# Starting a 7-product block inside the output projection, with respaced attention steps and an earlier first down pass

## The chip, the core and the metric

The kernel runs on one core of a Trainium2 chip. The metric is the device time of one execution in microseconds. The core has TensorE (PE in the profile, its weight loads PEld), VectorE (DVE), ScalarE (ACT), GpSimd (POOL) and SyncE (SP, which here only issues DMAs). Each engine works through a queue of its own, and semaphores tie the queues together.

## The reference

Two decoder layers over 256 tokens of width 2048, all in float32. Cut to what matters:

```python
h = rms_norm(x, norm1_g[l])
z = h @ w_in[l]                              # 2048 x 3584: sgu u | sgu v | q | k | v
out_a = chunked_sgu(gelu(z_sgu), ...)        # 16 groups, 128 x 128 causal mixing per chunk
out_b = swa_sink_attention(q, k, v, ...)     # 16 heads, 4 key heads, window 128, sinks, bias
mixed = concat([rms_norm(out_a), rms_norm(out_b)])
x = x + mixed @ w_out[l]                     # 2048 x 2048
h2 = rms_norm(x, norm2_g[l])
x = x + (silu(h2 @ w_gate[l]) * (h2 @ w_up[l])) @ w_down[l]   # 2048 x 5632 twice, 5632 x 2048
```

## The kernel before

The 256 tokens are two tiles of 128 (t = 0, 1). Weights come in pieces of 256 rows by 512 columns, 512 KB each, into one of 7 buffers named raw. Each piece is split into two float32r parts: ACT casts the high part wh (L94, 5 buffers), DVE subtracts to get the low part wl (L95, 4 buffers). Every product is then three matmuls (mm3, L124 to L126): high by high, high by low, low by high.

An **ordinary unit** (`unit`, L128) is one piece against both token tiles: 12 matmuls of 512 columns. A **7-product unit** (`s_unit` in `seven`, L608) is one piece in a Strassen-like scheme for gate and up: 6 matmuls. Here a 2 x 2 arrangement of token halves and gate/up column blocks is computed in seven products instead of eight, for feed-forward blocks 1 to 10 of 11. A 7-product block has 28 units and 30 steps (a step is one `yield`). Its first 20 units come in four groups i = 0 to 3 of five; each group needs three pieces, three DVE additions (L636, L637, L640) and one accumulating load by POOL (L642) into the tile t2. Group i uses the transposed, normed activations pairs2[2i] and pairs2[2i+1], and the sums of them in ext2. The block accumulates in five PSUM tiles of pool pa (tag acc, named m in the profile). At its end come ACT and DVE steps that undo the scheme, the gating (`gated`, L659), and the transposes of the result (`act_T`, L584, named ps_f, then aT).

PSUM is shared by three pools: pa with 5 slots (tag acc), pd with 2 (tag dacc) and pm with 1. Small products and transposes take their slots by turns from pm, pd, pd, pa (`small_ps`, L119).

The order in which instructions are written is set by hand. `tick` (L107) advances a clock, by 1 for an ordinary unit and by 0.5 for a 7-product unit; `later(delay, fn)` (L104) runs fn at the first tick at or after its due time, and things due at one tick go by due time, then by the order of registration. The framework then plans each engine's queue from that written order and its own estimates, so instructions can run ahead of their written place.

A layer goes so:

- The input projection, seven blocks of 8 ordinary units, in the order k and v, two blocks of q, two of sgu v, two of sgu u. Between the units, by `later`, run the norms of k and q (`head_inv`, with a power on POOL, L171), their transposes (`to_T`), six attention pieces (`attend`, L322, at ticks 6, 9, 12, 15, 19 and 23 after the first q block), each with scores ps_s, then exps one tick later, then `turn` (transposes ps_p) three ticks later, then `weigh` (ps_v, then ob) five ticks later; the closing transposes of a head group (`attend_end`), and the spatial gate (`spatial`).
- The output projection, eight parts of four units (`add_part`, L555), in the order b0, b1, a0, a1, b2, a2, b3, a3: b is the attention half of the input, a the sgu half, the figure the block of 512 columns. Each accumulates in pa; DVE then adds the scaled result into xres (L559). After an a part the block's squares and transposes for the next norm follow (`norm_block`, L500, and `combine`, L474).
- The feed-forward: `s_stream` runs the ten 7-product blocks step by step, and `std_stream` (L785) offers ordinary units: gate and up of block 0 (`gate_up`, 16 units in pd), and passes of `down` over finished blocks, 8 units for each block. A loop at L802 puts ordinary units between the steps, 88 in 300 steps. `down` seeds its accumulators with xres (L721), multiplies, and drains them into xres (L746). It starts a pass when at least two finished blocks are there, or all that are left.

Of the kernel before, what the change touches and what calls it, by code (L numbers as in the profile page):

```python
# [20 lines left out]
P = 128  # L21
# [42 lines left out]
def trunk(ctx, tc, x, xt, w_in, w_out, w_gate, w_up, w_down, sgu_w, sgu_g, consts,  # L64
# [182 lines left out]
    for lay in range(L):  # L247
# [40 lines left out]
        def q_norm(b, acc, lay=lay, layer=layer, qT=qT):  # L288
            qn = []
            for t in range(NTOK):  # L290
                z = zp.tile([P, NB], F32, tag="z", name="zq")
                nc.scalar.activation(z, acc[t], AF.Copy, scale=layer["rstd1"][t])
                qn.append(z)

            def scaled(inv):
                for t in range(NTOK):
                    z3 = qn[t].rearrange("p (h d) -> p h d", d=HD)
                    nc.vector.tensor_tensor(z3, z3, bc(inv[t], HD), ALU.mult)
# [12 lines left out]

        ssb = small([P, NTOK, 2], "ssb")
        ob = {}
# [8 lines left out]
        def attend(gp, t, i0, n, zkv=zkv, kT=kT, qT=qT, ob=ob, bias=bias, layer=layer):  # L322
# [229 lines left out]
        pairs2 = []  # L552
        ext2 = []

        def add_part(n, pairs, chunks, kind):  # L555
            acc = product([w_out[lay, n, c] for c in chunks], pairs)
            for t in range(NTOK):
                xs = xres[:, t, n * NB : (n + 1) * NB]
                nc.vector.scalar_tensor_tensor(  # L559
                    xs, acc[t], rstds[kind][t], xs, ALU.mult, ALU.add  # L560
                )

        for part, n in (("b", 0), ("b", 1), ("a", 0), ("a", 1), ("b", 2), ("a", 2), ("b", 3), ("a", 3)):
            if part == "b":
                add_part(n, pairs_b, range(4, 8), part)
            else:
                add_part(n, pairs_a, range(4), part)
                norm_block(n, ss2, pairs2, lay, C_G2, ext2)
        rstd2 = finish_rms(ss2, D)

        nr = small([P, NTOK], "nr")
        nrstd2 = [nr[:, t : t + 1] for t in range(NTOK)]

        def negate(rstd2=rstd2, nrstd2=nrstd2):
            for t in range(NTOK):
                nc.vector.tensor_scalar(nrstd2[t], rstd2[t], -1.0, None, ALU.mult)

        later(2, negate)

        ss1 = small([P, NTOK, ND], "ss4")  # L580
        pairs1 = []
        pairs_f = {}
# [22 lines left out]

                later(2 + c, ready)

        def seven(b, lay=lay, pairs2=pairs2, ext2=ext2, act_later=act_later):  # L608
            bank = [pa.tile([P, NB], F32, tag="acc", name=f"m{i}") for i in range(5)]

            def s_unit(raw, m, i, op, first, last, bank=bank):
# [45 lines left out]
                nc.vector.tensor_tensor(out, x, y, ALU.add)  # L657

            def gated(t, psum, sg, c):  # L659
                nc.scalar.activation(sg, psum, AF.Silu, scale=rstd2[t])  # L660
                nc.vector.scalar_tensor_tensor(sg, c, nrstd2[t], sg, ALU.mult, ALU.mult)

            steps = {
                0: lambda: add(c21, bank[2], m0),
# [19 lines left out]
                yield from seven(b)  # L684

        seeds = []

        def even(b, w, lay=lay, pairs2=pairs2):
            acc = new_acc(pd, "dacc")
# [4 lines left out]
                    yield True  # L694
            return acc

        def gate_up(b, even=even, act_later=act_later, seeds=seeds):
            acc = yield from even(b, w_gate)
            sg = []
            for t in range(NTOK):  # L700
                s = zp.tile([P, NB], F32, tag="z", name="sg")
                nc.scalar.activation(s, acc[t], AF.Silu, scale=rstd2[t])
                sg.append(s)
            acc = yield from even(b, w_up)
            for t in range(NTOK):
                nc.vector.scalar_tensor_tensor(
                    sg[t], acc[t], rstd2[t], sg[t], ALU.mult, ALU.mult
                )
                later(1.5 + 0.5 * t, lambda t=t: seeds[0](0, t))
            act_later(b, sg)  # L710

        left = [NFF]

        accs = {}
        full = {}
# [69 lines left out]
        def std_stream(gate_up=gate_up, down=down, pairs_f=pairs_f, left=left):  # L785
            gus = list(GU_BLOCKS)
            downed = set()
            while left[0]:
                full = [b for b in sorted(pairs_f) if len(pairs_f[b]) == 2 and b not in downed]
                rest = left[0] == len(full)  # L790
                if len(full) >= CHUNK[0] or rest:
                    blocks = full[: CHUNK[1]]
                    downed.update(blocks)
                    yield from down(blocks)
# [2 lines left out]
                else:  # L797
                    yield False

        other = std_stream()  # L800
# [98 lines left out]
```

## Time and profile before

| | |
|---|---|
| median of 3 runs | 1940.1 us (1939.55 to 1940.67) |
| the profiled execution | 1940.95 us |
| its span, first to last instruction | 1939.2 us |
| PE busy | 1925.2 us (99%) |
| DVE busy | 1660.9 us (86%) |
| ACT busy | 1301.4 us (67%) |
| POOL busy | 123.2 us (6%) |
| DMA | 426.41 MB, 220 GB/s in the mean |
| mean granted clock of TensorE | 0.999 |

The busy time of PE is modelled from the starts of its matmuls, and the share is a mean over stages. A group's row gives line, engine, operation, output from inputs, shape and count, then busy us and mean ns of one, then the engine's idle time just before it and what ended it. A row of a timeline gives start and length in us, and in brackets the idle time before and its releaser. A row of a table of stretches gives the stretch, its length and for each engine busy us and instructions, then the granted clock as a share, the DMA engines' busy share and GB/s.

### The profile page before, as it was taken

Reading aid. Unit: us, or ns where it says so; the run is one execution under the profiler, and the core shown is the slowest. Engines: PE = TensorE matmul, PEld = TensorE weight load, DVE = VectorE, ACT = ScalarE, POOL = GpSimd, SP = SyncE. Lnnn points to the kernel's source line nnn. Section 1 sums busy time; section 2 is a strip of 40 time slices with the busy share of each in tenths; the row PEclk is TensorE's granted clock in tenths of the full one; section 3 lists DMA queues with packets and bytes.
Section 4 is the critical chain, followed back from the end, with each engine's and each line's share of the span. In section 5 each row is a group of like instructions: output and inputs, shape, how many; then the busy total and the mean of one; then the engine's idle time right before and its main releaser. Section 6 shows DMA issues by size and latency. Waiting matters only on the chain.

```text
span 1939.2 us, 25050 instructions
## 1 busy us (share of the span) xinstructions
PE 1925.2 (99%) x8836; PEld 1578.4 (81%) x8836; DVE 1660.9 (86%) x1752; ACT 1301.4 (67%) x1729; POOL 123.2 (6%) x124
## 2 busy tenths in 40 slices
PE   9999999999999999999999999999999999999999
PEld 7888887878888888888887888878788888888887
DVE  6666689999999999999556666899999999999993
ACT  7665566667766776767755655666677767767675
POOL 1210000000000000000002000000000000000000
PEclk9999999999999999999999999999999999999999
DMA  9644558667867787777655445586678677876783
GB/s 369 201 145 158 183 168 259 215 212 243 277 212 239 225 274 213 243 238 256 196 201 192 133 163 176 176 265 209 212 237 286 208 240 226 269 218 234 238 264 125
DMA packets 118958, 426.41 MB, mean 220 GB/s; under 512 B 13232, under 2 KB 13872, under 8 KB 118832
## 3 DMA queue, kind: packets, MB, share of 16 engines
q1 hardware_dynamic: 105264, 375.52, 53.3%
q0 software_dynamic: 13568, 49.29, 14.2%
q8 instruction: 69, 1.13, 0.2%
q14 instruction: 57, 0.47, 0.1%
HBM read 422.66 MB, written 2.10 MB: 219 GB/s over the span
## 4 chain that ended last, share of the span: by engine, by line
PE 94%; issue 2%; DVE 2%; ACT 1%; POOL 0%; DMA 0%; SPq 0%; ACTq 0%; DVEq 0%; POOLq 0%
PE m L125 13%; PE m L124 13%; PE m L126 13%; PE acc L124 9%; PE acc L126 9%; PE acc L125 9%; PE dacc L125 8%; PE dacc L124 8%; PE dacc L126 8%; PE ps_f L188 1%; DVE wl L95 1%; PE ps_v L381 1%; PE ps_n L188 1%; PE ps_s L332 1%; PE ps_t L188 0%
## 5 line engine op out<-in xcount | busy, mean ns | idle before, releaser
L94 ACT CAST wh<-raw 128x1024 fp32r<-128x1024 f32 (+1 forms) x786 | 804.1, 1049 | 455.2 <-DVE raw L636 167.4
L95 DVE TENSOR_TENSOR wl<-raw,wh 128x1024 fp32r<-128x1024 f32 (+1 forms) x786 | 936.0, 1220 | 159.5 <-PE acc L125 98.8
L124 PE MATMUL m<-wh,ext 128*128 128x512 f32 x640 | 251.9, 395 | 0.6 <-ACT wh L94 0.6
L125 PE MATMUL m<-wl,ext 128*128 128x512 f32 x640 | 251.8, 393 | 0.7 <-DVE wl L95 0.6
L126 PE MATMUL m<-wh,ext 128*128 128x512 f32 x640 | 250.2, 391 | 0.0
L124 PE MATMUL dacc<-wh,aT 128*128 128x512 f32 x576 | 224.7, 391 | 0.9 <-ACT wh L94 0.9
L125 PE MATMUL dacc<-wl,aT 128*128 128x512 f32 x576 | 224.5, 390 | 0.1
L126 PE MATMUL dacc<-wh,aT 128*128 128x512 f32 x576 | 224.3, 389 | 0.0
L95 DVE TENSOR_TENSOR wl<-t,wh 128x1024 fp32r<-128x1024 f32 x160 | 194.1, 1222 | 3.7 <-issue 1.7
L94 ACT CAST wh<-t 128x1024 fp32r<-128x1024 f32 x160 | 167.9, 1052 | 38.3 <-DVE t L637 12.8
L125 PE MATMUL m<-wl,hT 128*128 128x512 f32 x480 | 187.2, 390 | 0.0
L126 PE MATMUL m<-wh,hT 128*128 128x512 f32 x480 | 186.8, 389 | 0.0
L124 PE MATMUL m<-wh,hT 128*128 128x512 f32 x480 | 186.5, 389 | 0.0
L124 PE MATMUL acc<-wh,hT 128*128 128x512 f32 x448 | 179.7, 402 | 1.3 <-ACT wh L94 1.3
L125 PE MATMUL acc<-wl,hT 128*128 128x512 f32 x448 | 175.5, 392 | 0.3 <-DVE wl L95 0.3
L126 PE MATMUL acc<-wh,hT 128*128 128x512 f32 x448 | 175.8, 392 | 0.0
L642 POOL DMA_DIRECT2D t<-in_w_gate_dram x80 | 68.4, 855 | 1331.3 <-DVE wl L95 1126.9
L124 PE MATMUL acc<-wh,aT 128*128 128x512 f32 x384 | 151.6, 395 | 0.0
L126 PE MATMUL acc<-wh,aT 128*128 128x512 f32 x384 | 150.0, 391 | 0.0
L125 PE MATMUL acc<-wl,aT 128*128 128x512 f32 x384 | 149.5, 389 | 0.0
L125 PEld LDWEIGHTS m<-wl,ext 128*128 128x128 f32 x640 | 120.2, 188 | 32.6 <-DVE wl L95 8.5
L124 PEld LDWEIGHTS m<-wh,ext 128*128 128x128 f32 x640 | 120.2, 188 | 27.0 <-ACT wh L94 2.6
(138 smaller groups left out, 2704.2 us busy)
## 6 DMA issues: line engine op xcount, KB each, us to landing
raw<-in_w_gate_dram SPq DMA_DIRECT2D x176, 512.0 KB, 5.8
raw<-in_w_up_dram SPq DMA_DIRECT2D x176, 512.0 KB, 5.6
raw<-in_w_down_dram SPq DMA_DIRECT2D x176, 512.0 KB, 5.0
raw<-in_w_in_dram SPq DMA_DIRECT2D x108, 512.0 KB, 4.2
t<-in_w_gate_dram POOLq DMA_DIRECT2D x80, 512.0 KB, 5.8
raw<-in_w_out_dram SPq DMA_DIRECT2D x64, 512.0 KB, 3.3
bias<-in_band_dram POOLq DMA_DIRECT2D x8, 512.0 KB, 4.8
xr<-in_xt_dram SPq DMA_DIRECT2D x8, 256.0 KB, 5.6
```

Source lines behind the costliest of these rows:

```text
L94: nc.scalar.copy(wh[:, j : j + step, :], src)
L95: nc.vector.tensor_tensor(wl[:, j : j + step, :], src, f(wh[:, j : j + step, :]), ALU.subtract)
L124: nc.tensor.matmul(acc, ah, wh, start=first, stop=False, skip_group_check=again)
L125: nc.tensor.matmul(acc, ah, wl, start=False, stop=False, skip_group_check=again)
L126: nc.tensor.matmul(acc, al, wh, start=False, stop=last, skip_group_check=again)
L188: nc.tensor.transpose(ps[:, j, t * P : (t + 1) * P], blocks[t][:, j * P : (j + 1) * P], ident)
L332: nc.tensor.matmul(ps[r][:, i, :], qT[gp][rows, i0 + i, t * P : (t + 1) * P], kT[rows, gp, :nk], start=True, stop=True,)
L381: nc.tensor.matmul(pv[:, r, i], pt[:, (r * n + i) * (t + 1) + b, :], zkv[b][:, cols], start=b == 0, stop=b == t,)
L642: nc.gpsimd.dma_start(t2, w_gate[lay, b, i, 1], accum_op=ALU.add)
```

## The change

1. The transposes of a q block come 3 and 5 ticks after it (before 4 and 5); `turn` comes after 2.95 ticks instead of 3, and so ahead of an attend piece that is due at the same tick; the two halves of `spatial` come after 5 and 8 ticks (before 6 and 7), the two closing transposes of a head group after 6 and 8 (before 6 and 7).
2. `add_part` becomes a generator that yields after each unit. The last two parts, b3 and a3 (eight units), accumulate in pd instead of pa, and five steps of the first 7-product block (LEAD) are written between those eight units. The loop that mixes ordinary units into the steps then counts from there: 88 in 295 steps.
3. The norm factors rstd2 and their negatives are made after these eight units and reach `gated` and `gate_up` through a dictionary norm2.
4. The first pass of `down` starts on one finished block; later ones on two, as before. The early seeding after `gate_up` is left out when a pass has already begun.

```diff
+LEAD = 5
             for c in range(2):
-                later(4 + c, lambda c=c: to_T(c))
+                later(3 + 2 * c, lambda c=c: to_T(c))
             later(1, exps)
-            later(3, turn)
+            later(2.95, turn)
             later(5, weigh)
             for half in range(2):
-                later(6 + half, lambda half=half: spatial(half))
+                later(5 + 3 * half, lambda half=half: spatial(half))
                 for r in range(2):
-                    later(at + 6 + r, lambda gp=gp, r=r: attend_end(gp, r))
+                    later(at + 6 + 2 * r, lambda gp=gp, r=r: attend_end(gp, r))
-        def add_part(n, pairs, chunks, kind):
-            acc = product([w_out[lay, n, c] for c in chunks], pairs)
+        def add_part(kind, n, pool=pa, tag="acc"):
+            pairs, base = (pairs_b, 4) if kind == "b" else (pairs_a, 0)
+            acc = new_acc(pool, tag)
+            for c in range(4):
+                unit(
+                    w_out[lay, n, base + c], [(pairs[c], 0), (pairs[c], 1)], acc, c == 0, c == 3
+                )
+                yield
             for t in range(NTOK):
                 xs = xres[:, t, n * NB : (n + 1) * NB]
                 nc.vector.scalar_tensor_tensor(
                     xs, acc[t], rstds[kind][t], xs, ALU.mult, ALU.add
                 )
+            if kind == "a":
                 norm_block(n, ss2, pairs2, lay, C_G2, ext2)
...
+        for kind, n in (("b", 0), ("b", 1), ("a", 0), ("a", 1), ("b", 2), ("a", 2)):
+            for _ in add_part(kind, n):
+                pass
+
+        def last_parts():
+            for kind in ("b", "a"):
+                yield from add_part(kind, ND - 1, pd, "dacc")
+
+        norm2 = {}
...
-                later(1.5 + 0.5 * t, lambda t=t: seeds[0](0, t))
+                later(1.5 + 0.5 * t, lambda t=t: left[0] < NFF or seeds[0](0, t))
...
-                if len(full) >= CHUNK[0] or rest:
+                if len(full) >= (CHUNK[0] if downed else 1) or rest:
...
+        steps = s_stream()
+        k = 0
+        for u, _ in enumerate(last_parts()):
+            while k * 8 < (u + 1) * LEAD:
+                next(steps)
+                k += 1
+        rstd2 = finish_rms(ss2, D)
...
         other = std_stream()
         done = 0
-        for k, _ in enumerate(s_stream()):
-            while done * HALVES < (k + 1) * (STD_UNITS - TAIL) and next(other, False):
+        for _ in steps:
+            k += 1
+            while done * (HALVES - LEAD) < (k - LEAD) * (STD_UNITS - TAIL) and next(other, False):
                 done += 1
```

More of the change, by code (lines that the diff above doesn't have):

```diff
@@ L561, in add_part @@
                 )
[L563 to L567, printed above, removed]
-                norm_block(n, ss2, pairs2, lay, C_G2, ext2)
[L569 to L578, printed above, removed]
+            if kind == "a":
+                norm_block(n, ss2, pairs2, lay, C_G2, ext2)
+        for kind, n in (("b", 0), ("b", 1), ("a", 0), ("a", 1), ("b", 2), ("a", 2)):
[5 more added lines that the diff above has]
+        norm2 = {}
         ss1 = small([P, NTOK, ND], "ss4")
@@ L606, in act_later, with seven @@
                 later(2 + c, ready)
-        def seven(b, lay=lay, pairs2=pairs2, ext2=ext2, act_later=act_later):
+        def seven(b, lay=lay, pairs2=pairs2, ext2=ext2, act_later=act_later, norm2=norm2):
             bank = [pa.tile([P, NB], F32, tag="acc", name=f"m{i}") for i in range(5)]
@@ L659, in gated @@
             def gated(t, psum, sg, c):
-                nc.scalar.activation(sg, psum, AF.Silu, scale=rstd2[t])
-                nc.vector.scalar_tensor_tensor(sg, c, nrstd2[t], sg, ALU.mult, ALU.mult)
+                nc.scalar.activation(sg, psum, AF.Silu, scale=norm2["r"][t])
+                nc.vector.scalar_tensor_tensor(sg, c, norm2["n"][t], sg, ALU.mult, ALU.mult)
             steps = {
@@ L686, in trunk @@
         seeds = []
+        left = [NFF]
         def even(b, w, lay=lay, pairs2=pairs2):
@@ L695, in even, with gate_up @@
             return acc
-        def gate_up(b, even=even, act_later=act_later, seeds=seeds):
+        def gate_up(b, even=even, act_later=act_later, seeds=seeds, left=left, norm2=norm2):
             acc = yield from even(b, w_gate)
@@ L701, in gate_up @@
                 s = zp.tile([P, NB], F32, tag="z", name="sg")
-                nc.scalar.activation(s, acc[t], AF.Silu, scale=rstd2[t])
+                nc.scalar.activation(s, acc[t], AF.Silu, scale=norm2["r"][t])
                 sg.append(s)
@@ L706, in gate_up @@
                 nc.vector.scalar_tensor_tensor(
-                    sg[t], acc[t], rstd2[t], sg[t], ALU.mult, ALU.mult
+                    sg[t], acc[t], norm2["r"][t], sg[t], ALU.mult, ALU.mult
                 )
-                later(1.5 + 0.5 * t, lambda t=t: seeds[0](0, t))
+                later(1.5 + 0.5 * t, lambda t=t: left[0] < NFF or seeds[0](0, t))
             act_later(b, sg)
-        left = [NFF]
         accs = {}
@@ L798, in std_stream, with negate @@
                     yield False
+        steps = s_stream()
[5 more added lines that the diff above has]
+        rstd2 = finish_rms(ss2, D)
+        nr = small([P, NTOK], "nr")
+        norm2["r"] = rstd2
+        norm2["n"] = [nr[:, t : t + 1] for t in range(NTOK)]
+        def negate(norm2=norm2):
+            for t in range(NTOK):
+                nc.vector.tensor_scalar(norm2["n"][t], norm2["r"][t], -1.0, None, ALU.mult)
+        later(2, negate)
         other = std_stream()
         done = 0
-        for k, _ in enumerate(s_stream()):
-            while done * HALVES < (k + 1) * (STD_UNITS - TAIL) and next(other, False):
+        for _ in steps:
+            k += 1
+            while done * (HALVES - LEAD) < (k - LEAD) * (STD_UNITS - TAIL) and next(other, False):
                 done += 1
```

## The prediction

> **What bounds the kernel now.** I read the page first, its span and busy line.
>
> ```profile
> span 1939.2 us, 25050 instructions
> ...
> PE 1925.2 (99%) x8836; PEld 1578.4 (81%) x8836; DVE 1660.9 (86%) x1752; ACT 1301.4 (67%) x1729; POOL 123.2 (6%) x124
> ```
>
> TensorE (PE) is the bound, and the change removes no matmul. So it can only win the time in which PE waits or runs slowly. Then I read a table of stretches of 20 us, looking for rows where PE is not full, or its clock not 1.00. Columns: stretch, length, busy us (instructions) of PE, weight loads, DVE, ACT, POOL, then clock, DMA share, GB/s.
>
> ```profile
> 300.00:320.00 20.00, 19.98 (x87) 15.65 (x86) 19.93 (x19) 9.56 (x10) 1.74 (x2) 1.00 0.83 221
> 320.00:340.00 20.00, 19.69 (x86) 15.72 (x85) 19.96 (x21) 15.21 (x16) 0.84 (x1) 1.00 0.91 327
> ...
> 400.00:420.00 20.00, 18.75 (x85) 14.34 (x84) 19.79 (x21) 13.38 (x18) 0.00 (x0) 1.00 0.45 164
> ...
> 1040.00:1060.00 20.00, 17.85 (x103) 14.29 (x102) 14.86 (x23) 13.02 (x25) 7.64 (x5) 0.99 0.50 153
> 1060.00:1080.00 20.00, 20.00 (x113) 16.77 (x112) 9.52 (x17) 11.61 (x34) 1.09 (x1) 0.92 0.47 162
> 1080.00:1100.00 20.00, 18.93 (x106) 15.80 (x106) 14.98 (x25) 15.43 (x30) 3.50 (x2) 1.00 0.34 105
> ...
> 1360.00:1380.00 20.00, 19.56 (x89) 15.56 (x87) 19.79 (x23) 13.54 (x17) 0.00 (x0) 1.00 0.62 227
> 1380.00:1400.00 20.00, 19.19 (x86) 15.33 (x86) 19.37 (x19) 12.59 (x16) 0.85 (x1) 1.00 0.73 223
> ```
>
> Beside the first 14 us and the last 5 us these are nearly all the holes: the start of the 7-product blocks (300 to 340), their first shortage of other work (around 411, and around 1379 in layer 2), and the attention of layer 2 (1054 to 1090). DVE is full in the first and second kind.
>
> **The second hole.** The timeline of PE shows its length. A 512-column matmul follows the last after 0.23 us.
>
> ```profile
> 410.62 0.40 PE L126 MATMUL m<-wh,hT 128*128 128x512 f32 x1
> 411.46 0.33 PE L188 MATMUL ps_f<-ident,m 128*128 128x128 f32 x1 [0.44 <-DVE aT L589]
> 411.72 0.50 PE L124 MATMUL m<-wh,ext 128*128 128x512 f32 x1
> 412.67 0.73 PE L124 MATMUL dacc<-wh,aT 128*128 128x512 f32 x2 [0.45 <-ACT wh L94]
> 413.73 0.50 PE L125 MATMUL m<-wl,ext 128*128 128x512 f32 x1 [0.32 <-DVE wl L95]
> ```
>
> Three steps take 0.84, 0.95 and 1.06 us where 0.23, 0.23 and 0.45 would do: 1.94 us lost. Layer 2 lacks the same (0.44 + 0.81 us of PE in its two rows, 1.25 in layer 1). The cause shows in stretches that count only instructions on the accumulators of the ordinary units (dacc):
>
> ```profile
> 385.20:398.80 13.60, 5.76 (x25) 4.50 (x24) 0.00 (x0) 0.00 (x0) 1.00 0.87 281
> 399.20:412.60 13.40, 0.00 (x0) 0.00 (x0) 1.41 (x2) 1.18 (x2) 1.00 0.38 154
> ```
>
> For 13.4 us PE has no ordinary unit. By the loop at L802 one ordinary unit follows 300/88 = 3.4 steps. Block 0's gate and up are 16 units, used up near step 54; block 1's pair is ready soon after step 30, but L791 asks for two full blocks, and block 0's pair comes only two and three ticks after its last unit. A 7-product unit gives PE 6 matmuls, 1.36 us, and needs 1.6 DVE operations in its first 20 units (three additions for five). With
>
> ```profile
> L636 DVE TENSOR_TENSOR raw<-raw 128x1024 f32<-128x1024 f32 x80 | 97.9, 1224 | 1.8
> ```
>
> that is up to 1.96 us of DVE for 1.36 of PE: without ordinary units (12 matmuls, 2.72 us, one DVE operation) DVE is the slower.
>
> **The change part by part.**
>
> *First down pass on one full block.* At the end of gate and up, block 1 is full, so its 8 units start at once and cover the time until blocks 0 and 2 are full. Passes go from 2,2,2,2,2,1 blocks to 1,2,2,2,2,2: still six, so as many seeds (L721) and drains (L746), none added. Gain 2 x 1.9 = 3.8 us.
>
> *Turn at 2.95, ends two ticks apart.* The hole in layer 2's attention:
>
> ```profile
> 1055.95 0.60 PE L369 MATMUL ps_p<-ident,s 128*128 128x128 f32 x4
> 1058.70 0.63 PE L369 MATMUL ps_p<-ident,s 128*128 128x128 f32 x4 [2.15 <-DVE s L337]
> 1059.09 0.48 PE L124 MATMUL acc<-wh,hT 128*128 128x512 f32 x1
> ```
>
> ```profile
> 1050.48 0.69 DVE L298 TENSOR_TENSOR zq<-zq,ir 128x512 f32<-128x512 f32 x1 [2.73 <-POOL ir L171]
> ...
> 1057.88 1.27 DVE L337 SCALAR_TENSOR_TENSOR s<-ps_s,bias 128x512 f32<-128x512 f32 x2
> ```
>
> At that tick the scores of unit 2 are issued before the turn of unit 1. Counting the calls of small_ps, the second ps_p gets the pool slot (pd) that the first ps_s has just filled, and must wait until DVE has read it, late because DVE stood 2.73 us behind the POOL power. Lost: 2.75 - 0.39 = 2.4 us. Then PE runs slowly:
>
> ```profile
> 1059.10:1063.50 4.40, 4.40 (x15) 3.41 (x13) 1.60 (x4) 2.76 (x10) 0.28 (x1) 0.61 0.93 277
> ```
>
> Twelve matmuls, one unit, take 4.4 us where 2.7 would do: 1.7 us lost at a clock of 0.61. With 2.95 the turn precedes the scores, ps_p gets slots (pa, pm) read long ago, and the scores get slots read by ob and qT a tick earlier. I take both back: 4.1 us. The Trainium skill (TensorE: Matmul & The Clock Gate, Part 1: The HAM clock gate) says the clock falls after an idle window of about 3.4 us; here 2.15 us of idleness, with small matmuls around it, sufficed. By that page the 1.7 us would not belong to the wait and the forecast would be 1.7 us later; the trace disagrees, so I keep it in.
>
> The third row of that stage:
>
> ```profile
> 1087.52 0.60 PE L188 MATMUL ps_t<-ident,ob 128*128 128x128 f32 x4
> 1089.19 0.49 PE L332 MATMUL ps_s<-kT,qT 64*128 64x256 f32 x2 [1.07 <-DVE aT L179]
> ```
>
> Here attend_end's ps_t fills the slot that the scores of the same tick need. With ends at 6 and 8 and the turn ahead, the scores get slots read by ob and by the copy of ps_p. Gain 1.1 us.
>
> *First transpose of q one tick earlier, the second and spatial respaced.* The risk is that zq isn't ready.
>
> ```profile
> 1022.33 1.29 DVE L298 TENSOR_TENSOR zq<-zq,ir 128x512 f32<-128x512 f32 x2 [2.79 <-POOL ir L171]
> ```
>
> ```profile
> 1026.30 0.60 PE L188 MATMUL ps_t<-ident,zq 128*128 128x128 f32 x4
> ...
> 1049.75 1.89 PE L381 MATMUL ps_v<-zkv,pt 128*128 128x64 f32 x16
> 1051.45 0.48 PE L124 MATMUL acc<-wh,hT 128*128 128x512 f32 x1
> ```
>
> A tick before 1026.30 is 1023.57, and zq ends at 1023.62: 0.1 us. For the second q block the new place is behind ps_v, at 1051.45; its first zq ends at 1050.48 + 0.69 = 1051.17, and a second of like length behind it near 1051.85: 0.4 us. Cost 0.5, bounds 0 and 1.5. Spatial moves from 6 to 5 and from 7 to 8: the norm chain behind it uses the same POOL power as zq, so I take 0, at worst the same 0.4 twice.
>
> *The block begins between the last eight units.* Five steps, after output units 1, 2, 4, 5 and 7, in each layer: 30 matmuls, 5 casts, 5 wl, 3 additions, three 512 KB loads on the SP queue (w_gate, two of w_up), and one accumulating load on POOL. All exist before; they only come earlier. SP: of 7 raw slots the group holds three, so the output units have four, 4 x 2.72 = 10.9 us ahead of use against 3.3 us to landing; POOL: one issue ahead of the norm's power, which is needed only after the gate's 8 units. Both cost nothing; with that cover gone, a load would be late by its landing time:
>
> ```profile
> t<-in_w_gate_dram POOLq DMA_DIRECT2D x80, 512.0 KB, 5.8
> ...
> raw<-in_w_out_dram SPq DMA_DIRECT2D x64, 512.0 KB, 3.3
> ```
>
> What it should win is DVE time: five steps' DVE work (8 operations) moves to where DVE has room, out of 300:340. There PE has 87 + 86 matmuls in 40 us, 176 at full pitch: 3 x 0.23 = 0.7 us a layer, 1.4 in all. Bounds: 0 (DVE prefetch ran ahead already) and 3.
>
> What it adds is a wait. The last eight units now accumulate in pd, which has two slots: unit 5 can begin only when DVE has added unit 4's two results into xres, and the gate likewise after unit 8. One step (1.36 us) lies between, and half a unit (0.68): 2.04 us of cover. DVE needs
>
> ```profile
> L559 DVE SCALAR_TENSOR_TENSOR xres<-acc,ir,xres 128x512 f32<-128x512 f32 x32 | 23.1, 747 | 6.4 <-PE acc L126 6.4
> ```
>
> 0.75 us, behind at most one wl of 1.22: 1.97. I take 0.1 for each of four handovers, 0.4. Queued behind it on DVE are the next wl; who waits for those is PE, four buffers later. The idle column says that DVE was waiting for PE at these additions, not late. The far bound is in rival three.
>
> *Sum.* 3.8 + 4.1 + 1.1 + 1.4 = 10.4 won, 0.5 + 0.4 = 0.9 paid: 9.5. The profiled execution took 1940.95 (span 1939.2), 0.85 above the median of 1940.1. 1940.95 - 9.5 = 1931.45, or 1930.6 against the median; I say 1931.
>
> **The rivals.**
>
> *One: ACT's order, not the missing units, makes the hole at 411.* ACT stood still there:
>
> ```profile
> 409.51 0.69 ACT L660 ACTIVATE c<-m,ir 128x512 f32<-128x512 f32 x1 [3.47 <-PE m L126]
> ```
>
> The casts behind L660 wait for a PE result. If that order stays, 3.8 us stay: 1934.8, with a little lost besides 1936. Against: ordinary units were missing too, and in the row from 385.20, where they ran, PE had no such gap. The Trainium skill (PSUM — Partial Sum Buffer, Engine vs sequencer instructions) calls ScalarE's queue strictly first in, first out, which is this rival; the trace agrees by the 3.47 us.
>
> *Two: the end of each layer opens instead.* By step 300 the 88 units asked for are exactly block 0's 16 and nine blocks of 8. Blocks 9 and 10 then wait for block 10's transposes, and three ticks pass in the written order without a unit. If PE keeps to that, it idles from the last m matmul until c is gated and the pairs are split:
>
> ```profile
> 903.34 0.58 ACT L721 COPY acc<-xres 128x512 f32<-128x512 f32 x1
> ...
> 922.78 0.69 ACT L660 ACTIVATE c<-m,ir 128x512 f32<-128x512 f32 x1 [0.24 <-PE m L126]
> ...
> 929.17 0.58 ACT L588 CAST aT<-ps_f 128x512 fp32r<-128x512 f32 x1
> ```
>
> ```profile
> 923.90 0.75 DVE L661 SCALAR_TENSOR_TENSOR c<-c,nr,c 128x512 f32<-128x512 f32 x1
> ...
> 929.79 0.69 DVE L589 TENSOR_TENSOR aT<-ps_f,aT 128x512 fp32r<-128x512 f32 x1 [0.51 <-ACT aT L588]
> ```
>
> From 922.6 to 924.65, and 0.58 + 0.69 again between the two pairs (one slot): 3.3 us, with 1.7 for the clock 5 us a layer: 1941. Against: the order of the queues isn't the written one. The seed at 903.34 belongs to the tail after the blocks and ran 20 us early, so block 9's units, whose pairs are long ready, should fill the hole.
>
> *Three, slower: the handovers in pd wait behind a full DVE.* DVE runs such rows:
>
> ```profile
> 303.96 4.63 DVE L95 TENSOR_TENSOR wl<-raw,wh 128x1024 fp32r<-128x1024 f32 x4
> ```
>
> Behind four wl an addition ends 4.63 + 0.75 us after its matmul: 3.3 us beyond the cover, 5 with the clock; four times, 20: 1951. It decides for slower once a handover costs over (1944.0 - 1931)/4 = 3.2 us. For it: the five steps fill just this stage's DVE. Against: the L559 row.
>
> **How the numbers follow.** A measurement of this kernel can tell about 0.2%, 3.9 us. Forecast: 0.60 (its own range 1927 to 1936, from the bounds). Rival one, or the attention hole surviving elsewhere: 0.15 at 1936, a third of it faster, the rest same. Rival two: 0.10 at 1941, mostly same. Rival three: 0.15 at 1951. Faster 0.65, same 0.18, slower 0.17. Low end 1926.5: the sum with 3 us for the block start, no costs and a little more; the high end of 1942 takes in rivals one and two and leaves rival three out.
>
> **What would show it.** Right: dacc matmuls in the 13.4 us after gate and up; no PE wait of over 1 us for s or aT in layer 2's attention, and no stretch below clock 1.00 there; PE full in the 40 us after the output projection. Wrong: PE idle before an output or gate unit with L559 as releaser (three), before ps_f at a layer's end (two), or before m with ACT wh as releaser at the first block's end (one).

## The result and the profile after

The changed kernel takes 1934.84 us (median of 8 runs, 1934.45 to 1936.16), the kernel before 1940.01 (8 runs beside it): a ratio of 0.9974, with a 95% interval of 0.9965 to 0.9984. That is 5.2 us, where 9.5 were forecast. The profiled execution took 1934.89 us, 6.1 less than that of before. The page of the changed kernel, its span and busy line:

```profile
span 1933.2 us, 25021 instructions
...
PE 1924.8 (100%) x8836; PEld 1576.6 (82%) x8836; DVE 1660.3 (86%) x1752; ACT 1306.6 (68%) x1733; POOL 125.4 (6%) x124
```

PE has as many matmuls as before and nearly the same busy time; what went is idle time. The same stretches of the changed kernel (length, busy us and instructions of PE, weight loads, DVE, ACT, POOL, then clock, DMA share, GB/s), with a long one through the middle of the first layer's feed-forward:

```profile
300.00:320.00 20.00, 20.00 (x90) 15.89 (x89) 19.92 (x25) 12.77 (x17) 0.89 (x1) 1.00 0.67 221
320.00:340.00 20.00, 19.99 (x88) 15.91 (x87) 19.85 (x21) 15.66 (x17) 0.85 (x1) 1.00 0.88 296
400.00:420.00 20.00, 20.00 (x96) 16.43 (x95) 19.45 (x20) 14.87 (x21) 0.85 (x1) 1.00 0.48 141
1040.00:1060.00 20.00, 20.00 (x115) 16.36 (x114) 15.60 (x24) 13.38 (x27) 6.63 (x7) 1.00 0.64 231
1060.00:1080.00 20.00, 20.00 (x124) 17.20 (x123) 9.35 (x17) 15.64 (x38) 1.09 (x1) 1.00 0.36 126
1080.00:1100.00 20.00, 20.00 (x113) 16.42 (x113) 15.87 (x27) 15.09 (x30) 3.50 (x2) 1.00 0.40 133
...
1360.00:1380.00 20.00, 20.00 (x94) 16.42 (x92) 19.46 (x20) 14.72 (x20) 0.86 (x1) 1.00 0.45 142
1380.00:1400.00 20.00, 19.85 (x90) 15.91 (x89) 19.93 (x20) 14.22 (x19) 0.86 (x1) 1.00 0.76 233
...
465.00:880.00 415.00, 414.44 (x1846) 340.22 (x1845) 403.05 (x377) 288.96 (x335) 22.18 (x26) 1.00 0.72 233
```

The long stretch in the kernel before:

```profile
465.00:880.00 415.00, 414.92 (x1850) 341.02 (x1849) 404.96 (x379) 291.38 (x337) 22.18 (x26) 1.00 0.74 237
```

Every hole that the prediction listed is full, but for 0.15 us in the last row of layer 2, with the clock at 1.00, and there are more matmuls in each: 90 and 88 from 300 to 340 for 87 and 86, 96 for 85 around 411. The long stretch shows the opposite: four matmuls fewer in the same 415 us, and DVE with two operations fewer. It is a stretch that nobody had aimed at.

PE's waits over the whole execution say the same of the holes. Columns: us in total, times, the longest. First the changed kernel, then the longest of the kernel before.

```profile
PE heat L155 <- DVE mhalf L157: 1.5, 1, 1.5
PE dacc L125 <- ACT wh L95: 0.6, 2, 0.3
PE acc L125 <- ACT wh L95: 0.5, 1, 0.5
PE acc L126 <- DVE wl L96: 0.3, 1, 0.3
PE m L126 <- DVE wl L96: 0.2, 1, 0.2
```

```profile
PE ps_p L369 <- DVE s L337: 2.1, 1, 2.1
...
PE ps_s L332 <- DVE aT L179: 1.1, 1, 1.1
PE dacc L124 <- ACT wh L94: 0.9, 2, 0.4
PE ps_f L188 <- DVE aT L589: 0.9, 2, 0.4
```

What these views can't show is the many small delays, each below what counts as a wait. For that the starts of all matmuls were taken, and from each step between two starts the usual step for these two kinds in the kernel before was subtracted. The sums by stage, in us that PE lost (this table is worked out, no view prints it; "in-projection" ends with the first 24 output units, "start" is the stretch from there up to the 540th matmul of 512 columns, "hole" the next 400 of these, "middle" the next 1800, "tail" the rest of the layer):

| kernel | in-projection 1 / 2 | start 1 / 2 | hole 1 / 2 | middle 1 / 2 | tail 1 / 2 |
|---|---|---|---|---|---|
| before | 6.33 / 10.79 | 2.67 / 2.69 | 2.97 / 2.99 | 3.51 / 3.29 | 0.86 / 0.16 |
| after | 7.03 / 6.01 | 1.68 / 1.79 | 1.32 / 1.33 | 5.09 / 5.07 | 1.60 / 0.44 |
| e1 attention only | 7.18 / 6.36 | 2.71 / 2.68 | 3.01 / 2.93 | 3.54 / 3.25 | 0.86 / 0.16 |
| e2 first pass only | 6.98 / 10.36 | 2.66 / 2.66 | 2.35 / 2.03 | 3.46 / 3.08 | 1.62 / 0.46 |
| e3 early steps only | 7.71 / 10.29 | 1.65 / 1.68 | 3.05 / 3.07 | 5.29 / 5.35 | 1.59 / 0.46 |
| e4 all but early steps | 7.73 / 6.02 | 2.66 / 2.67 | 1.98 / 2.07 | 3.41 / 3.11 | 1.60 / 0.44 |
| e5 old mixing | 7.01 / 6.01 | 2.42 / 2.42 | 2.02 / 2.04 | 3.51 / 3.16 | 1.62 / 0.45 |
| e6 one addition less | 7.50 / 6.01 | 1.15 / 1.14 | 0.43 / 0.42 | 1.36 / 1.33 | 1.60 / 0.46 |
| e10 mixing by load | 8.19 / 5.99 | 1.25 / 1.21 | 0.68 / 0.69 | 1.91 / 1.95 | 1.48 / 0.32 |
| e11 turn only | 8.28 / 6.77 | 2.65 / 2.65 | 2.99 / 2.96 | 3.80 / 3.22 | 0.85 / 0.16 |
| e12 as e10, no early steps | 6.82 / 5.99 | 1.14 / 1.14 | 1.79 / 1.79 | 2.32 / 2.29 | 1.45 / 0.33 |

From before to after: 4.8 won in layer 2's in-projection, 3.3 in the two holes, 1.9 in the two starts, together 10.0; 3.4 lost in the two middles, 1.0 in the tails, 0.7 in the first in-projection, which varies from kernel to kernel. That leaves 4.9, about 1 us less than the 6.1 between the profiled executions. The plain times between the same matmuls, with nothing subtracted, close: 5.9 shorter in layer 2's in-projection, of which the tail before it gives back 1.4, 3.2 in the holes, 1.9 in the starts, 0.2 before the first matmul; 3.4 longer in the middles, 0.2 in the last tail and 0.2 in the first in-projection. So layer 2's in-projection and the tail before it win 4.6 together. The forecast won its 10 us and lost some 4 to 5 of them, most in a place that it had not priced.

### The profile page after: what moved, and what is told of

Same layout as the page of the kernel before. It is cut to its first block, busy times and chain, and to the rows that moved or that the text cites. A ratio compares the mean times of both kernels' runs of the same rounds, so it can differ in the third digit from the quotient of the medians.

```text
span 1933.2 us, 25021 instructions
## 1 busy us (share of the span) xinstructions
PE 1924.8 (100%) x8836; PEld 1576.6 (82%) x8836; DVE 1660.3 (86%) x1752; ACT 1306.6 (68%) x1733; POOL 125.4 (6%) x124
## 4 chain that ended last, share of the span: by engine, by line
PE 95%; DVE 2%; issue 1%; ACT 1%; DMA 0%; SPq 0%; ACTq 0%; DVEq 0%
PE m L126 12%; PE m L127 12%; PE m L125 12%; PE acc L125 9%; PE acc L127 9%; PE acc L126 9%; PE dacc L125 9%; PE dacc L126 9%; PE dacc L127 9%; DVE wl L96 2%; PE ps_v L382 1%; PE ps_f L189 1%; ACT wh L95 1%; PE ps_s L333 1%; PE ps_t L189 1%
## 5 line engine op out<-in xcount | busy, mean ns | idle before, releaser
L126 PE MATMUL dacc<-wl,aT 128*128 128x512 f32 x640 | 249.8, 390 | 0.3
L125 PE MATMUL dacc<-wh,aT 128*128 128x512 f32 x640 | 249.2, 392 | 0.8 <-ACT wh L95 0.6
L127 PE MATMUL dacc<-wh,aT 128*128 128x512 f32 x640 | 249.3, 389 | 0.0
L125 PEld LDWEIGHTS dacc<-wh,aT 128*128 128x128 f32 x640 | 119.8, 188 | 29.4 <-ACT wh L95 3.6
L126 PEld LDWEIGHTS dacc<-wl,aT 128*128 128x128 f32 x640 | 120.2, 188 | 26.6 <-DVE wl L96 1.5
L127 PEld LDWEIGHTS dacc<-wh,aT 128*128 128x128 f32 x640 | 120.2, 188 | 24.9
```

The costliest lines, as they stand in the source:

```text
L125: nc.tensor.matmul(acc, ah, wh, start=first, stop=False, skip_group_check=again)
L126: nc.tensor.matmul(acc, ah, wl, start=False, stop=False, skip_group_check=again)
L127: nc.tensor.matmul(acc, al, wh, start=False, stop=last, skip_group_check=again)
```

## The experiments

The runs e1 to e4 share a chip (before: 1940.34 us), e5 to e8 (1940.64), e9 to e11 (1940.51); e12 ran beside a before of 1940.62.

**e1 to e4: the parts alone.** e1 has the four attention delays and nothing else:

```diff
-                later(4 + c, lambda c=c: to_T(c))
+                later(3 + 2 * c, lambda c=c: to_T(c))
...
-            later(3, turn)
+            later(2.95, turn)
...
-                later(6 + half, lambda half=half: spatial(half))
+                later(5 + 3 * half, lambda half=half: spatial(half))
...
-                    later(at + 6 + r, lambda gp=gp, r=r: attend_end(gp, r))
+                    later(at + 6 + 2 * r, lambda gp=gp, r=r: attend_end(gp, r))
```

> Only the four attention delays (q transposes, turn, spatial, closing transposes); output projection and feed-forward as before. Both theories: the hole at 1056 to 1063 and the one at 1088 in layer 2 go, about 4.8 us won there, some 0.7 us paid in layer 1, so 4.1 us faster than before, near 1936. Nothing changes in the feed-forward: the hole at 411 stays, of the same 1.9 us.

Measured: 1936.77 us, 0.9982 (0.9973 to 0.9991), 3.6 us less than before. The in-projection of layer 2 loses 4.4 us less, and no other stage of layer 2 moves by more than 0.1. The forecast for these steps was 4.1 + 1.1 - 0.5 = 4.7. Layer 1's in-projection loses 0.85 more than before; in this execution the clock stood at 0.50 from 7.7 to 11.1 us, where that of before was at 1.00.

e2 has only the first down pass on one full block:

```diff
-                if len(full) >= CHUNK[0] or rest:
+                if len(full) >= (CHUNK[0] if downed else 1) or rest:
...
-                later(1.5 + 0.5 * t, lambda t=t: seeds[0](0, t))
+                later(1.5 + 0.5 * t, lambda t=t: left[0] < NFF or seeds[0](0, t))
```

> Only the first down pass on one full block. Theory 1 (DVE is co-bound in the feed-forward, so a hole closed at 411 opens again in small waits later in the same layer): under 1 us a layer is left, 0 to 2 us faster in all. Theory 2 (the small waits come from the block's earlier start and the 88 in 295 mixture): 1.6 us a layer is kept, 3.3 us faster in all, near 1936.7, and the stretch from 465 to 880 is as in the kernel before.

Measured: 1939.7 us, 0.9997 (0.9988 to 1.0005): no difference that can be told, where the prediction's step gives 3.8. The hole shrinks only from 2.97 to 2.35 (layer 1) and from 2.99 to 2.03. In e2's timeline of PE the three gaps at 411 are gone, but a new one stands behind them; ACT's timeline shows where it is from (start, length, then in brackets the idle time before and its releaser):

```profile
417.24 0.27 PE L188 MATMUL ps_f<-ident,m 128*128 128x128 f32 x1
418.40 0.50 PE L124 MATMUL dacc<-wh,aT 128*128 128x512 f32 x1 [0.89 <-ACT wh L94]
```

```profile
413.67 0.59 ACT L745 COPY xres<-dacc 128x512 f32<-128x512 f32 x1 [4.04 <-PE dacc L126]
...
417.29 1.06 ACT L94 CAST wh<-raw 128x1024 fp32r<-128x1024 f32 x1
```

ACT stood still for 4 us before the drain of an accumulator, which waits for PE; the casts behind it in its queue came late, and PE then waited 0.89 us for one of them. This is the mechanism of the prediction's rival one, at another instruction: the drain of the pass that was put there to fill the hole.

e3 has only the early steps, with the mixing that belongs to them:

```diff
+        for u, _ in enumerate(last_parts()):
+            while k * 8 < (u + 1) * LEAD:
+                next(steps)
+                k += 1
...
-        for k, _ in enumerate(s_stream()):
-            while done * HALVES < (k + 1) * (STD_UNITS - TAIL) and next(other, False):
+        for _ in steps:
+            k += 1
+            while done * (HALVES - LEAD) < (k - LEAD) * (STD_UNITS - TAIL) and next(other, False):
```

> Only the five steps between the last eight output units; first down pass on two blocks, attention as before. Theory 1: the start of the feed-forward gains 1 us a layer, the hole at 411 stays, and the five steps' DVE work taken out of the stage is kept, so 2 to 4 us faster. Theory 2: the small waits of the long middle (465 to 880) appear here too, 1.7 us a layer, and eat the 1 us: 0 to 2 us slower.

Measured: 1943.05 us, 1.0013 (1.0004 to 1.0022), 2.7 us slower than before. The starts are 1.0 us shorter in each layer, a little more than the 0.7 of the forecast, but the middles lose 5.3 us each where before lost 3.4. In the long stretch of e3 are fewer matmuls still:

```profile
465.00:880.00 415.00, 414.57 (x1845) 339.97 (x1844) 402.20 (x376) 288.29 (x332) 22.18 (x26) 1.00 0.73 234
```

So the 3.4 us that after loses in the middles come with this part of the change.

e4 is the changed kernel without the early steps, so e1 and e2 together.

> Attention delays and first down pass on one block, no five steps. Theory 1: about the attention's 4.1 us and little more, 1935 to 1936, slower than or equal to the changed kernel's 1934.8. Theory 2: 4.1 + 3.3 = 7.4 us faster than before, near 1932.6, so faster than the changed kernel.

Measured: 1934.71 us, 0.9972 (0.9961 to 0.9983), the same as the whole change. The part that gave the change its name is worth nothing in sum: in layers 1 and 2 it wins 1.0 and 0.9 us at the start and 0.7 and 0.7 in the hole, and gives 1.7 and 2.0 back in the middle.

**e5: the mixing, with the early steps kept.** The ordinary units are again 88 in 300 steps, counted from the block's own first step; as the first five steps lie in the output projection, two units come together at step 6 of the first block and one more at step 7:

```diff
-            while done * (HALVES - LEAD) < (k - LEAD) * (STD_UNITS - TAIL) and next(other, False):
+            while done * HALVES < k * (STD_UNITS - TAIL) and next(other, False):
```

> The changed kernel, but ordinary units are again put between the steps at 88 in 300, counted from the block's first step, so that from step 6 on each ordinary unit stands behind the same step as before the change. Theory 2 (the small waits of the middle come from where ordinary units fall among a block's steps, which 88 in 295 makes almost the same in each block: 8.95 units a block in place of 8.8): the middle goes back to that of the kernel before, 1.7 us a layer are won, 3.4 in all, near 1931.4. Theory 3 (they come from the block's earlier start itself): the middle stays, 1934.8.

Measured: 1933.6 us, 0.9965 (0.9951 to 0.9978). The middles go from 5.09 and 5.07 back to 3.51 and 3.16, within 0.2 the values of before. The early steps alone don't bring the loss, then; it goes with how the ordinary units fall on a block's steps. But the start goes from 1.68 to 2.42 and the hole from 1.32 to 2.02: what the middle wins is mostly given back there, and the time is 1.2 us below after's, with overlapping intervals.

**e6 and e7: is DVE the limit behind it?** In e6 one DVE addition of three in each group is left out, in e7 it is made twice:

```diff
                 yield
-                nc.vector.tensor_tensor(b12, b12, b22, ALU.add)
                 s_unit(t2, 3, i, e_op(2), first, last)
```

> The changed kernel with one of the three DVE additions of each group (b12 + b22) left out, so the product that uses that sum is computed from b12 alone. If the remaining waits of the feed-forward are for DVE at the groups' starts, 2 to 3 us a layer go, 1929 to 1931. If they come from the order of ACT alone, nothing changes: 1934 to 1935.

> The changed kernel with that addition done twice, so the same product is computed from b12 + 2 b22: 40 more DVE operations of 1.13 us a layer, 45 us. DVE is idle for about 16 us of the 620 us of a layer's blocks. If DVE is at its limit, PE waits for the rest, some 25 to 30 us a layer: 1985 to 1995. If PE has enough stored, under 10 us in all.

Measured: e6 1924.79 us (0.992, 0.9906 to 0.9933), e7 2008.33 us (1.035, 1.0331 to 1.0369). By their pages DVE is busy for 1583.8 and 1751.7 us, 76.5 less and 91.4 more than in after. The 76.5 us less are worth 10 us of the time, the 91.4 more cost 73.5; both are more than was expected. The long stretch of e6, then of e7:

```profile
465.00:880.00 415.00, 415.00 (x1858) 343.31 (x1857) 381.65 (x354) 292.86 (x339) 22.18 (x26) 1.00 0.75 237
```

```profile
465.00:880.00 415.00, 402.29 (x1744) 319.70 (x1743) 409.56 (x384) 275.18 (x322) 20.48 (x24) 1.00 0.74 229
```

With 33 us of room on DVE, PE is full (1858 matmuls for 1846). With 12 us, as in after, it loses some 5 us a layer; with the addition doubled, DVE sets the pace. The feed-forward is at the edge between the two engines, and time in which DVE stands still can cost PE a part of it. Most of the loss of the middle (5.1 to 1.4) goes when DVE's load goes.

**e8 and e9: the same addition elsewhere.** In e8 POOL makes it, in e9 an accumulating load of the same weights does:

```diff
-                nc.vector.tensor_tensor(b12, b12, b22, ALU.add)
+                nc.gpsimd.tensor_tensor(b12, b12, b22, ALU.add)
```

```diff
+                nc.gpsimd.dma_start(b12, w_up[lay, b, i, 1], accum_op=ALU.add)
...
-                nc.vector.tensor_tensor(b12, b12, b22, ALU.add)
```

> The changed kernel with that addition on POOL instead of DVE: the result is the reference's. If the waits are for DVE and POOL is quick enough (its idle share is over 90%), as with the addition left out: 1929 to 1931. If POOL takes several us for it and the piece comes late, or slows DVE, slower than 1935.

> The changed kernel with the third addition of each group made by a second accumulating load (b22's piece is added into b12 by the DMA engines) instead of DVE; the result is the reference's, 42 MB more are moved. If DVE is what PE waits for in the feed-forward, as with the addition left out: 1925 to 1928. If the longer way of b12 (issue, load, add) makes its unit late in each group, PE waits there instead: over 1935.

Measured: e8 2045.14 us (1.0539, 1.0524 to 1.0554), e9 1983.12 us (1.022, 1.0206 to 1.0235). Groups of e8 (busy us, mean ns of one, then the idle time before and what ended it):

```profile
L641 POOL TENSOR_TENSOR raw<-raw 128x1024 f32<-128x1024 f32 x80 | 276.3, 3454 | 870.8 <-DVE raw L637 794.0 <-DMA raw<-in_w_out_dram 60.4 <-DMA raw<-in_w_up_dram 16.4
...
L638 DVE TENSOR_TENSOR t<-raw 128x1024 f32<-128x1024 f32 x80 | 127.2, 1590 | 2.1
```

POOL takes 3.45 us for what DVE does in 1.22, and DVE's own addition at L638, which stands beside it in each group, goes from 1.22 to 1.59. With 80 additions taken off DVE, the kernel is 110 us slower than after; PE's longest wait there is for wl, 48.4 us in 37 times. In e9 it is the loads (waits of ACT, and the landing time of the accumulating load of t2):

```profile
ACT wh L95 <- DMA raw<-in_w_up_dram: 130.5, 59, 5.0
```

```profile
t<-in_w_gate_dram POOLq DMA_DIRECT2D x80, 512.0 KB, 8.6
```

After has no such wait of ACT among its largest, and its t2 lands in 5.7 us. The casts now wait for loads. Neither way off DVE pays with these buffers.

**e10: ordinary units where DVE is loaded.** An ordinary unit gives PE 2.72 us of work for one DVE operation, so it should stand in a block's first 20 steps, where the additions are. The count of 88 stays, with weights of 1.15 for these steps and 0.7 for the last ten:

```diff
+        def even_at(k):
+            r = k % 30
+            return 30 * (k // 30) + 1.15 * min(r, 20) + 0.7 * max(r - 20, 0)
...
-            while done * (HALVES - LEAD) < (k - LEAD) * (STD_UNITS - TAIL) and next(other, False):
+            while done * (HALVES - even_at(LEAD)) < (even_at(k) - even_at(LEAD)) * (STD_UNITS - TAIL) and next(other, False):
```

> The changed kernel with the same 88 ordinary units, but put more densely into a block's first 20 steps, where DVE has 8 operations for 5 units, and more thinly into its last 10 (weights 1.15 and 0.7). Theory 2 in the form that waits come where ordinary units are too thin beside the groups: the middle's 5.1 us fall to about 2.5 a layer, near 1930. If only the repetition of one pattern in each block matters, the middle stays near 5, 1934 to 1936.

Measured: 1927.21 us, 0.993 (0.9917 to 0.9942): 13.3 us below before and 7.6 below after, and the fastest here that leaves nothing out. Followed through the loop, the ordinary units now come after every second or third step up to step 20 or 21, and then after every fourth or fifth; half of the blocks have seven of them in their first 20 steps, where in before and after each has six (after's first block five). The long stretch:

```profile
465.00:880.00 415.00, 414.92 (x1855) 342.72 (x1854) 405.74 (x379) 289.94 (x336) 22.20 (x26) 1.00 0.74 236
```

Nine matmuls more than after in the same 415 us, and no operation removed from the kernel. DVE's waits in that stretch, in after and then in e10, show what changed:

```profile
DVE wl L96 <- issue: 3.1, 4, 1.2
DVE wl L96 <- ACT wh L95: 2.4, 5, 1.0
DVE wl L96 <- PE dacc L126: 2.0, 2, 1.0
DVE wl L96 <- PE dacc L127: 1.4, 1, 1.4
```

```profile
DVE wl L96 <- issue: 3.1, 6, 1.1
DVE wl L96 <- ACT wh L95: 3.0, 9, 1.0
```

In after DVE waits three times, 3.4 us in all, for PE at an ordinary unit (before has two such waits, 2.0 us): DVE has run ahead there and stands still until a wl buffer is free. In e10 these waits are gone. That it lacks just this time in the next group of additions would fit the gain of e10, but the waits are no measure of the loss: e3 has the same two waits as before, 2.0 us in each layer, and its middles lose 5.3 where those of before lose 3.4. Nor is DVE's idle time as a whole: by the rows above DVE stands still for 9.3 us of the stretch in e10, for 10.0 in before. What counts is where the time is lacking, and these views show it only in part.

**e11: the turn alone.**

```diff
-            later(3, turn)
+            later(2.95, turn)
```

> The kernel before with the turn at 2.95 alone. If the hole at 1056 and the slow clock behind it come from the order of scores and turn at one tick, 2.4 + 1.7 us go and the wait at 1088 stays: 4.1 us faster, near 1936. If the closing transposes' spacing is needed too, the hole stays: 1940.

Measured: 1940.63 us, 1.0001 (0.9992 to 1.0009): no gain in the time, a miss by that measure. The profiled execution, at 1939.39 us, shows what happened. In layer 2 the step did its work: the in-projection loses 6.8 us instead of 10.8, and the stretch that had 15 matmuls at a clock of 0.61 is full:

```profile
1059.10:1063.50 4.40, 4.40 (x24) 3.69 (x23) 3.77 (x6) 2.60 (x8) 0.53 (x1) 1.00 0.93 326
```

But in layer 1 a new hole is there, which before does not have. Timelines of PE and DVE:

```profile
130.31 0.50 PE L125 MATMUL acc<-wl,hT 128*128 128x512 f32 x1 [1.02 <-DVE wl L95]
```

```profile
122.07 1.29 DVE L439 TENSOR_TENSOR v<-v,ir 128x512 f32<-128x512 f32 x2 [3.04 <-POOL ir L171]
...
129.04 1.22 DVE L95 TENSOR_TENSOR wl<-raw,wh 128x1024 fp32r<-128x1024 f32 x1
130.18 0.15 DVE L348 TENSOR_TENSOR es<-nm,nsink 128x4 f32<-128x4 f32 x1
130.25 1.22 DVE L95 TENSOR_TENSOR wl<-raw,wh 128x1024 fp32r<-128x1024 f32 x1
```

DVE waited 3.04 us for POOL's power in the norm of v, and then worked through the attention and gate operations that stand between before it came to the next wl. That wait for POOL is there in before and after as well, but at neither does PE then run out of wl. Another 0.9 us of that in-projection lies elsewhere, most of it between 80 and 100 us, where there are 110 matmuls for 115 in before. The turn's 4 us in layer 2 are seen in the trace; that they were spent again in layer 1 rests on one profiled execution, and the runs of this kernel scatter from 1938.99 to 1942.97.

**e12: e10's mixing without the early steps.**

```diff
-            while done * HALVES < (k + 1) * (STD_UNITS - TAIL) and next(other, False):
+            while done * HALVES < even_at(k + 1) * (STD_UNITS - TAIL) and next(other, False):
```

> The kernel of e4 (attention steps and first down pass changed, no step between the last eight output units) with the mixing of e10: 88 ordinary units in 300 steps, denser in the first 20 steps of a block. Theory one, that the placing of the ordinary units against the DVE load alone makes the gain of e10: the middle of the feed-forward falls to about 1.9 us lost per layer, the start of the blocks stays at 2.7, and the time is 1927.2 plus up to 2, 1927 to 1929.5. Theory two, that e10 needs the early start of the block too, since DVE then enters the block with its first loads split: the middle stays near 3.3, and the time is above 1931. If it is 1927 or below, the early start is worth nothing or less.

Measured: 1928.6 us, 0.9941 (0.9928 to 0.9955). Theory one has the time, and nearly the middle (2.3 for 1.9), but not all of its working: the start, expected at 2.7, falls to 1.14, as low as with the early steps. So the early steps aren't needed for the start; more ordinary units there do the same. What they do bring with this mixing is the hole, 0.7 for 1.8 us a layer, since without them the drain again holds up ACT:

```profile
415.83 0.50 PE L124 MATMUL dacc<-wh,aT 128*128 128x512 f32 x1 [0.55 <-ACT wh L94]
```

```profile
411.58 0.59 ACT L745 COPY xres<-dacc 128x512 f32<-128x512 f32 x1 [2.85 <-PE dacc L126]
```

By the whole table the early steps are worth 2.8 us in the two feed-forwards under this mixing. In the medians it is 1.4, with overlapping intervals on two chips; e10's first in-projection lost 1.4 more than e12's.

## Why the prediction was right and where it was not

**Turn, ends, transposes of q (4.7 us).** Right: 4.8 in after, 4.4 in e1 by the table, and 4.0 of it with the turn alone (e11), for which the prediction had 4.1. After has no ps_p or ps_s among PE's waits, and ps_p now stands ahead of the scores of the same tick:

```profile
1054.19 1.03 PE L370 MATMUL ps_p<-ident,s 128*128 128x128 f32 x8
1055.16 1.13 PE L333 MATMUL ps_s<-kT,qT 64*128 64x256 f32 x8
```

The 1.7 us at a low clock went with the wait, in after (1.00 in all three rows) and in e11, so they belonged to it. In before, narrower stretches show the clock at 0.50 for 3.4 us, which is 1.7 us of lost work, and PE busy for 1.25 us of the 3.4 us ahead of it:

```profile
1056.30:1059.70 3.40, 1.25 (x10) 0.96 (x9) 3.37 (x4) 1.35 (x3) 1.62 (x3) 1.00 1.02 358
1059.80:1063.20 3.40, 3.40 (x9) 2.63 (x9) 0.93 (x3) 2.32 (x10) 0.00 (x0) 0.50 0.86 274
```

The Trainium skill (TensorE: Matmul & The Clock Gate, Part 1: The HAM clock gate) asks for an idle window of about 3.4 us; in these traces a wait of 2.15 us beside small matmuls was enough, and waits of 1.07 us (before, at 1089) and 1.02 us (e11, at 130) were not.

**First pass on one block (3.8 us).** Right in sum and wrong as a step. After loses 3.3 us less in the two holes, and the accumulators of the ordinary units now have work in the 13.4 us that were empty:

```profile
399.20:412.60 13.40, 5.76 (x24) 4.50 (x24) 1.43 (x2) 1.10 (x2) 1.00 0.28 89
```

But e2 shows that this step alone closes 1.6 of 6.0 us, and with the attention steps (e4) 1.9; another 1.4 comes only with the early steps and their mixing, from which the prediction expected nothing here. That the sum came near 3.8 is luck. What stayed open is rival one's order on ACT, which the prediction had set against it at 0.15 as either one or the other; both were true at once. The Trainium skill (PSUM — Partial Sum Buffer, Engine vs sequencer instructions) has ScalarE's queue strictly in order; the 4.04 us before L745 in e2, with a cast waiting behind it, agree.

**Start of the block (1.4 us).** Right in size, 1.9. The reason is not shown: that it needs DVE work moved between the output units is not so, since e12's start is lower without it, and with the early steps under the old mixing (e5) the start wins only 0.3 a layer, though there the three units at steps 6 and 7 may cost some of it.

**Handovers in pd (0.4 us, rival three 1951).** Right to give the rival little. In the grouped lines of the changed kernel DVE's addition at L566 held up weight loads by 0.5 us in all, and no matmul:

```profile
L125 PEld LDWEIGHTS dacc<-wh,aT 128*128 128x128 f32 x640 | 119.8, 188 | 29.4 <-ACT wh L95 3.6 <-ACT dacc L721 0.6 <-DVE xres L566 0.5
```

**The end of a layer (rival two).** Did not occur. In PE's timeline of after, the last m matmul is followed without a gap by the tail's units:

```profile
921.41 0.39 PE L127 MATMUL m<-wh,hT 128*128 128x512 f32 x1
921.65 0.27 PE L189 MATMUL ps_f<-ident,m 128*128 128x128 f32 x1
921.67 0.47 PE L125 MATMUL acc<-wh,aT 128*128 128x512 f32 x1
```

The tails lose 0.7 and 0.3 us more than before, which e2, e3 and e4 have too. In e2 and e3, which leave the attention as it was, layer 2's in-projection behind the first of these tails loses 0.4 and 0.5 less, so part of it only moves across that border; what the rest is wasn't tried.

**The term that was missing.** The step that failed is the one on the five early steps: "All exist before; they only come earlier", priced at 1.4 won and 0.4 paid. The mixing that it brings along, 88 units in 295 steps for 88 in 300, was used for rival two and nowhere priced. It costs 3.4 us (e3 and e5 tie it to the mixing, e6 to DVE), and this is most of the distance between 9.5 and the 5.2 measured. That the time still lies in the forecast's own range, 1927 to 1936, is luck in this part: its high end was set for other costs. The prediction looked for stretches in which PE was not full; the middle, at 414.92 of 415 us, looked full, and had no room to lose by that reading. The row beside it, DVE busy for 404.96 of 415, was the one to read.

Which of the shifted units costs most can be told in part, by splitting the table's middle by block and by unit. The difference lies in blocks 7 to 10: there after loses 3.8 us in layer 1 and 3.9 in layer 2, before 2.2 and 2.0; ahead of them the middles lose 1.3 and 1.2 for 1.3 and 1.3. Within a block most of it stands at the 7th and the 13th 7-product unit, each with the ordinary unit that may follow it: 0.8 and 1.7 us in layer 1 for 0.1 and 0.5. The last eight units lose nothing in any of these kernels. Before, e5 and after have six ordinary units in a block's first 20 steps (after's first block five), and only their places differ. In after's blocks 7 to 10 they follow the 7-product units 3, 7, 10, 13, 17 and 20 or 4, 7, 10, 14, 17 and 20; in before the places move on from block to block. But before's block 5 has the first of these patterns and loses 0.5 us, where after's block 7 loses 1.1, so the places alone don't settle it, and why the loss grows there stays open.

## What to carry to other kernels

Where the second engine is busy for 97% of a stage, the stage has two bounds, and an edit that only reorders work can cost or win there as much as one that closes a visible hole: price the moved order against that engine too, group by group. Put the work that is light for the second engine where its load is densest; here that alone was worth 7.6 us (medians on two chips) with no instruction removed, more than the whole change. And a part that closes a hole by moving work into it must be followed through the in-order queues of every engine that serves that work, its drains included.

## What the runs showed of the hardware

An addition of two float32 tiles of 128 x 1024 took 1.22 us on DVE and 3.45 on POOL, and beside POOL's the other DVE addition of the group took 1.59. Made by accumulating loads instead, 42 MB more, it raised the landing time of the other accumulating loads from 5.7 to 8.6 us. After PE's wait of 2.15 us, in a stretch of 3.4 us with PE busy for 1.25, the clock stood at 0.50 for 3.4 us. Moving one step by 0.05 of a tick closed that hole in layer 2, and the one execution that was profiled has a new one of 1.02 us in layer 1, behind a wait of DVE for POOL that was there before without such a hole.
